# Two layers of a hybrid backbone: the S5 chunk tables' TensorE products issued as whole runs

## The chip, the cores and the metric

The kernel runs on one core of a Trainium2 chip. The metric is the device time of one execution in microseconds (us). A difference of about 0.5% (5.6 us) is what a measurement of this kernel can tell from no change.

## What is computed

Two layers of a backbone run on 384 tokens (128 of context, 256 of a latent grid) of width 1024. Each layer is a modulated RMS norm, one input projection, four parallel mixers, one output projection, a second norm and a gated MLP with a width-3 convolution:

```python
def trunk_layer(x, cvec, p, mixer_fn):
    sh1, sc1, g1, sh2, sc2, g2 = ada_mods(cvec, p)
    mixed, extra = mixer_fn(rmsnorm(x, p['norm1_g']) * (1 + sc1) + sh1)
    x = x + g1 * mixed
    x = x + g2 * conv_ffn(rmsnorm(x, p['norm2_g']) * (1 + sc2) + sh2, p)
    return x, extra

def mixers_context(h, p):
    na_z, s5_u, gq_z, mla_z = split_proj(h @ p['w_in'])
    o_na = attend(nq, nk, nv, NA_DH ** -0.5)
    o_s5, s5_state = s5_mixer(s5_u, p, ...)
    o_gq = attend(gq, gk, gv, GQ_DH ** -0.5)
    o_mla = attend(mq, mk, mv, MLA_QK ** -0.5)
    return concat(o_na, o_s5, o_gq, o_mla) @ p['w_out'], ...
```

The change touches the S5 mixer only: a state space of 16 channel groups with 64 complex states each, in two directions. The kernel computes it in chunks of eight tokens, which needs three tables per layer that depend on the weights alone: E (inputs of a chunk to its end state), F (start state to outputs) and KT (the lags inside a chunk).

## The kernel before

**Tiling.** Features lie on the 128 partitions, tokens on the free axis. Every large product is split in three products of single-pass floats (high by high, high by low, low by high), lines 295 to 297 in `mm3`: a weight tile of 128x128 against 384 or 386 columns. They fill the whole array of TensorE. The text calls them main products. Weights come in pieces by DMA; `split1` (lines 282 to 289) makes the high part on ScalarE (L287) and the low part on VectorE (L288), up to four half pieces of 512 columns ahead.

**Stages.** Layer 0: norm and first products, four mixers interleaved by the letters of `SPEC`, output projection, MLP in two halves of 11 pairs (`ffn`, lines 1310 to 1380). Then layer 1, the same. The S5 tables of layer 0 are made inside the mixers of layer 0, those of layer 1 inside the second MLP half of layer 0 (lines 1314 to 1322), at a lower priority (`LOWP`) than the MLP around them.

**The tables** (`s5_tables`, lines 687 to 734) are made in four blocks per layer. In each block VectorE makes `eb` by six operations (L491 to L500); TensorE transposes it twice (i = 0, 1) in four pieces of 128x128 (L707) into a PSUM tile, ScalarE copies it out (L708) and GpSimd's queue writes it to memory (L709). VectorE makes `ca` by six more operations (L491 to L498), which GpSimd's queue writes (L716). Then 16 products of 64 rows by 32 columns and 128 moving columns (L723) fill two PSUM tiles: four groups g on four strips of 32 columns, two directions d on the upper and lower 64 rows, and two parts i (real, imaginary) that are summed. The eight pairs of g and d stand on eight different corners of the array; i = 0 and i = 1 use the same corner one after the other. ScalarE (L727, L728) and VectorE (L729, L730) take the result to `KT`.

**Order.** Only the norm stage of layer 0 is written in its order by hand. Elsewhere a scheduler places the instructions of each engine in one fixed order at build time, by data dependences and priorities (`high_priority` raises one). The engines then run their orders and wait for each other by semaphores. `adjacent` (lines 242 to 247) traces the last of a list of products first and ties the others behind it with `issue_after`, so that they come after it; before the change it is used for column sums (L391, L903) and for the products of probabilities and values (L974, L978), and does not raise their priority.

**Small products beside these.** The modulation product (L318) uses 128 rows by 32 columns with 256 moving columns, four column strips at a time.

Of the kernel before, what the change touches and what calls it, by code (L numbers as in the profile page):

```python
# [34 lines left out]
PRL = 1000  # L35
PRX = 3000
NI = 0
NX = 5
# [177 lines left out]
def _program(tc, I, O):  # L216
# [25 lines left out]
    def adjacent(calls):  # L242
        """products of different column groups in a row, behind the last one"""
        calls[-1]()
        with tc.issue_after(nc.cur_bb.bb.instructions[-1]):
            for c in calls[:-1]:
                c()
# [90 lines left out]
    def step(n=1):  # L338
        """the next pieces of the modulation product"""
        for _ in range(n):  # L340
            if not ada_cur:
                if not ada_todo:
                    return
                ada_cur.append(ada_steps(*ada_todo[0]))
            next(ada_cur[0])
            left[0] -= 1
            if left[0] % 16 == 0:
                ada_cur.clear()
                ada_todo.pop(0)
# [10 lines left out]
    def rsqrt(src, scale, shape):  # L360
        """1 / sqrt(scale * src + EPS)"""
        xe = tiny(shape, "rs", 7)
        V.tensor_scalar(xe, src, scale, EPS, op0=OP.mult, op1=OP.add)
        xh = tiny(shape, "rs", 7)
        V.tensor_scalar(xh, xe, -0.5, None, op0=OP.mult)
        i = tiny(shape, "rs", 7, I32)
        V.tensor_scalar(i, xe.bitcast(I32), 1, None, op0=OP.logical_shift_right)
        yi = tiny(shape, "rs", 7, I32)
        V.tensor_scalar(yi, i, -1.0, float(0x5f3759df), op0=OP.mult, op1=OP.add)
        y = yi.bitcast(F32)  # L370
        for _ in range(3):
            t = tiny(shape, "rs", 7)
            V.tensor_tensor(t, y, y, op=OP.mult)
            V.tensor_tensor(t, t, xh, op=OP.mult)
            y2 = tiny(shape, "rs", 7)
            V.scalar_tensor_tensor(y2, t, 1.5, y, op0=OP.add, op1=OP.mult)
            y = y2
        return y
# [16 lines left out]
    def inv_rms(st, between=lambda i: None):  # L395
        """per token 1 / rms, the same on all rows of a psum tile"""
        ste = kp.tile([128, T], F32, name="ste", tag="sq", bufs=5)
        A.activation(ste, st[:, :T], AF.Copy)
        tr = pt()
        for b in range(3):  # L400
            PE.transpose(tr[:, 128 * b:128 * b + 128], ste[:, 128 * b:128 * b + 128], ident)
        ms = tiny((3,))
        V.tensor_reduce(ms, tr[:, :T].rearrange("p (b r) -> p b r", b=3)[:, :, 0:128:32], axis=AX.X, op=OP.add)
        A.activation(ms, ms, AF.Sqrt, scale=1.0 / D, bias=eps)
        between(0)
        r = tiny((3,))
        V.reciprocal(r, ms)
        between(1)
        bc = pt()
        for b in range(3):  # L410
            PE.transpose(bc[:, 128 * b:128 * b + 128], r[:, b:b + 1].to_broadcast([128, 128]), ident)
        return bc
# [23 lines left out]
    def unscaled(pool, tag, bufs, l, k, Am, sh):  # L436
        """x * gain in two parts, not yet over its rms, and the two shifts in columns behind it"""
        hi, lo = [pool.tile([128, 386], F32R, name="u" + t, tag=t, bufs=bufs) for t in tag]
# [11 lines left out]
    def scaled(out, z, bc, o1=0, o2=0):  # L450
        """product of unscaled() over the rms, with the shifts' product added; segment s at column o_s"""
        with tc.high_priority(offset=PRX):
# [16 lines left out]

# [1 line left out]
    lre, lim, ldt = s5p[:, 0], s5p[:, 1], s5p[:, 2]  # L471
# [35 lines left out]
    def par(*gens):  # L507
        """steps of independent chains in turn"""
        gens = list(gens)
# [7 lines left out]
    def s5_params(qp, rest):  # L517
        """powers of the discrete poles and input gains, one small instruction per step"""
        def tt(dt=F32, n=iter(range(99))):
# [126 lines left out]
    def s5_rot(l, w, w4, qp, cmp):  # L646
        """rotation by chunk position, decays, rotated entry states"""
        lg = slice(16 * l, 16 * l + 16)
# [38 lines left out]
    def s5_tables(l, qp, cmp, bc, dd):  # L687
        """chunk tables of one layer: E (inputs to end state), F (start state to outputs), lags inside a chunk"""
        lg = slice(16 * l, 16 * l + 16)
# [6 lines left out]
        for b in range(4):  # L696
# [6 lines left out]
            for i in range(2):  # L703
                e = kp.tile([128, 512], F32, name="tbo", tag="sqz", bufs=3)
                tr = pt()
                for g in range(4):
                    PE.transpose(tr[:, 128 * g:128 * g + 128], eb[:, i, g].rearrange("p j c -> p (j c)"), ident)  # L707
                A.activation(e, tr, AF.Copy)  # L708
                G.dma_start(SE[l][:, b, 512 * i:512 * i + 512], e)  # L709
# [8 lines left out]
            kd = [pt(), pt()]  # L718
            for d in range(2):
                h = slice(64 * d, 64 * d + 64)  # L720
                for i in range(2):
                    for g in range(4):
                        PE.matmul(kd[d][32 * g:32 * g + 32, 0:128], bb[i][h, 4 * b + g],  # L723
                                  ca[h, i, g, 2 * d:2 * d + 8].rearrange("p t c -> p (t c)"), start=i == 0,
                                  stop=i == 1)
            k4 = [k[:, 0:128].rearrange("p (t c) -> p t c", t=8) for k in kd]
# [9 lines left out]
    def s5_stream(l, st):  # L736
        """leaves 2 * gelu(y), channels on partitions, then the gated output"""
        with tc.tile_pool(name=f"sp{l}", bufs=1) as sp_:
# [160 lines left out]
    def stats(items, w=T):  # L899
        """column sums of squares; item c gives rows 32c.. by its weights; then [token, block, 32c + row]"""  # L900
        n = 32 * len(items)
# [16 lines left out]
    def softmax_unit(at, S, w, scale, bias, norm_act):  # L918
        """rows of exp(scale * S + bias - max) over their sum"""
        P = at.tile([128, T], F32, name="P", tag="P", bufs=3)  # L920
# [19 lines left out]
    def heads_stream(at, heads, res):  # L940
        """two heads, outputs on rows 0..63 and 64..127 of one tile, split in two parts"""
        PTs = []
# [44 lines left out]
    def kbroadcast(at, rr):  # L987
        """rr [128 tokens, block, 2] to rows of a psum tile, 64 rows each"""
        rb = at.tile([128, 3, 2, 64], F32, name="rb", tag="rp", bufs=1)
# [307 lines left out]
    def ahead(wsrc, n, H, zs, sts):  # L1297
        """first products of a stage from unscaled rows, then 1 / rms while they run"""
        bc = None
# [82 lines left out]
    def first(up, steps, rest):  # L1382
        """first layer: modulation, norm and the first products, rows k at a time; steps: DVE work between"""
        steps = [steps]
# [192 lines left out]
```

## Time and profile before

| what | value |
|---|---|
| time of three runs | 1115.03, 1115.62, 1119.07 us; median 1115.62 |
| profiled execution, first to last instruction | 1119.8 us (no other time is recorded for it) |
| TensorE busy | 1075.4 us, 96% of the span |
| VectorE busy | 803.6 us, 72% |
| ScalarE busy | 584.5 us, 52% |
| GpSimd busy | 86.0 us, 8% |
| DMA moved | 182.19 MB, 163 GB/s on average |

The span of the profiled execution is 4.2 us above the median of the runs. TensorE is the engine that is nearly always busy, but busy is not the same as doing useful work: the records of neighbouring products overlap, and the distance from the start of one product to the start of the next tells what it really costs. A record count of x2 for a small product (L723, L318) is one product in two passes, so x16 are eight products.

### The profile page before, as it was taken

The page shows a single profiled execution, that of the slowest core. Times are in us where ns is not written, and L with a number is a line of the kernel's source. Part 1 is how long each engine was busy: PE and PEld are TensorE (multiplying, and loading weights), DVE is VectorE, ACT ScalarE, POOL GpSimd, SP SyncE. Part 2 cuts the span into 40 slices and gives each one's busy share as a digit, 9 for nine tenths or more (in the row PEclk, how much of TensorE's full clock was granted, in tenths as well). Part 3 has the DMA queues.
Part 4 walks back from the last instruction along what each step waited for, and adds up shares of the span by engine and source line. Part 5 has one row for each costly group of instructions (what it writes and reads, how often), then busy time and mean ns, then how long its engine had stood idle before and what let it go on. Part 6 is the DMA issues. An engine that isn't in the chain of part 4 may idle for free.

```text
span 1119.8 us, 18705 instructions
## 1 busy us (share of the span) xinstructions
PE 1075.4 (96%) x6724; PEld 911.0 (81%) x6724; DVE 803.6 (72%) x2026; ACT 584.5 (52%) x1251; POOL 86.0 (8%) x197
## 2 busy tenths in 40 slices
PE   6789899999999999999999989899999999999998
PEld 3567575458889999996999887645699999999998
DVE  6888587867799854775976886567669875477753
ACT  3654445565675533552556644574567653355532
POOL 4213121000100000000010220000000000000000
PEclk8999899999999999998999998999999999999999
DMA  9978876464544444442455683336333434444343
GB/s 346 296 246 306 224 214 241 162 230 148 166 151 132 135 116 146 131 117 97 146 150 160 187 277 131 77 126 217 101 126 96 142 109 118 141 129 132 104 137 99
DMA packets 64700, 182.19 MB, mean 163 GB/s; under 512 B 15840, under 2 KB 19168, under 8 KB 64608
## 3 DMA queue, kind: packets, MB, share of 16 engines
q1 hardware_dynamic: 55456, 152.52, 44.0%
q0 software_dynamic: 8576, 28.16, 8.1%
q8 instruction: 53, 0.87, 0.3%
q10 hardware_dynamic: 576, 0.32, 0.1%
q14 instruction: 39, 0.32, 0.1%
HBM read 166.19 MB, written 14.78 MB: 162 GB/s over the span
## 4 chain that ended last, share of the span: by engine, by line
PE 67%; DVE 3%; DMA 1%; issue 1%; ACT 1%; POOL 0%; SPq 0%; DVEq 0%; POOLq 0%; ACTq 0%
PE pz L295 11%; PE pz L296 10%; PE pz L297 10%; PE psc L297 8%; PE psc L295 8%; PE psc L296 8%; PE pa L318 2%; PE psc L955 1%; PE ptr L723 1%; DMA bias<-rpb 1%; PE ptr L959 1%; DVE lo L288 1%; PE po L974 1%; PE psc L778 1%; DVE mg L798 0%
## 5 line engine op out<-in xcount | busy, mean ns | idle before, releaser
L287 ACT ACTIVATE hi<-raw 128x512 fp32r<-128x512 f32 (+2 forms) x396 | 228.3, 585 | 288.1 <-PE pz L296 120.0
L288 DVE TENSOR_TENSOR lo<-raw,hi 128x512 fp32r<-128x512 f32 (+2 forms) x396 | 252.6, 640 | 157.9 <-ACT hi L287 112.6
L295 PE MATMUL pz<-ah,hi 128*128 128x386 f32 (+1 forms) x616 | 216.3, 353 | 2.7 <-ACT ah L1439 1.7
L296 PE MATMUL pz<-al,hi 128*128 128x386 f32 (+1 forms) x616 | 213.7, 347 | 1.0 <-DVE al L426 1.0
L297 PE MATMUL pz<-ah,lo 128*128 128x386 f32 (+1 forms) x616 | 212.9, 346 | 0.1
L295 PEld LDWEIGHTS pz<-ah,hi 128*128 128x128 f32 x616 | 117.8, 191 | 21.6 <-issue 15.0
L296 PEld LDWEIGHTS pz<-al,hi 128*128 128x128 f32 x616 | 118.5, 192 | 7.0 <-issue 6.0
L297 PEld LDWEIGHTS pz<-ah,lo 128*128 128x128 f32 x616 | 118.0, 192 | 5.5 <-issue 4.4
L297 PE MATMUL psc<-ah,lo 128*128 128x386 f32 (+1 forms) x336 | 115.4, 343 | 0.1
L296 PE MATMUL psc<-al,hi 128*128 128x386 f32 (+1 forms) x336 | 115.1, 343 | 0.0
L295 PE MATMUL psc<-ah,hi 128*128 128x386 f32 (+1 forms) x336 | 115.1, 343 | 0.0
L295 PEld LDWEIGHTS psc<-ah,hi 128*128 128x128 f32 x336 | 64.1, 191 | 1.4 <-issue 1.0
L297 PEld LDWEIGHTS psc<-ah,lo 128*128 128x128 f32 x336 | 64.1, 191 | 0.9 <-DVE lo L288 0.4
L296 PEld LDWEIGHTS psc<-al,hi 128*128 128x128 f32 x336 | 64.0, 191 | 0.6 <-issue 0.6
L318 PE MATMUL pa<-raw,cw 128*32 128x256 f32 x640 | 59.1, 392 | 4.4 <-DMA raw<-ada 4.4
L295 PE MATMUL pz<-fh,hi 128*128 128x384 f32 x176 | 59.8, 340 | 0.0
L295 PE MATMUL psc<-fh,hi 128*128 128x384 f32 x176 | 59.4, 338 | 0.0
L297 PE MATMUL psc<-fh,lo 128*128 128x384 f32 x176 | 59.4, 337 | 0.0
L297 PE MATMUL pz<-fh,lo 128*128 128x384 f32 x176 | 59.3, 337 | 0.0
L296 PE MATMUL psc<-fl,hi 128*128 128x384 f32 x176 | 59.2, 336 | 0.0
L296 PE MATMUL pz<-fl,hi 128*128 128x384 f32 x176 | 59.1, 337 | 0.0
L932 ACT ACTIVATE P<-psc,ty 128x384 f32<-128x384 f32 (+1 forms) x56 | 32.3, 577 | 35.4 <-DVE ty L931 27.7
(431 smaller groups left out, 1959.7 us busy)
## 6 DMA issues: line engine op xcount, KB each, us to landing
raw<-wup SPq DMA_DIRECT2D x88, 512.0 KB, 3.6
raw<-ada SPq DMA_DIRECT2D x80, 512.0 KB, 4.5
raw<-win SPq DMA_DIRECT2D x30, 512.0 KB, 4.7
raw<-wdn SPq DMA_DIRECT2D x32, 384.0 KB, 3.1
raw<-wdn SPq DMA_DIRECT2D x32, 320.0 KB, 2.9
a<-ada SPq DMA_DIRECT2D x16, 512.0 KB, 6.2
raw<-wout SPq DMA_DIRECT2D x16, 512.0 KB, 3.7
se<-tbo POOLq DMA_DIRECT2D x16, 256.0 KB, 4.1
```

The lines of the kernel that those rows point to most:

```text
L287: A.activation(hi[:, :n], raw[:, a:b], AF.Copy)
L288: V.tensor_tensor(lo[:, :n], raw[:, a:b], hi[:, :n].bitcast(F32), op=OP.subtract)
L295: PE.matmul(out, wh, xh, start=start, stop=False)
L296: PE.matmul(out, wh, xl, start=False, stop=False)
L297: PE.matmul(out, wl, xh, start=False, stop=stop)
L318: PE.matmul(acc[32 * c:32 * c + 32, 256 * h:256 * h + 256], cw[:, kc], raw[:, 256 * c:256 * c + 256], start=kc == 0 and h == 0, stop=kc == ...
L723: PE.matmul(kd[d][32 * g:32 * g + 32, 0:128], bb[i][h, 4 * b + g], ca[h, i, g, 2 * d:2 * d + 8].rearrange("p t c -> p (t c)"), start=i == ...
L778: PE.matmul(e[:, NC * q:NC * q + NC], E[:, 128 * q:128 * q + 128], U[:, 4 * b + g], start=True, stop=True)
L932: A.activation(P[:, :w], S[:, :w], AF.Exp, bias=mx, scale=scale, accum_out=rs)
L955: PE.matmul(S[:, :T], qf(1 + qb), kf(128, 512), start=True, stop=True)
L959: PE.transpose(tr[:, 128 * kb:128 * kb + 128], P[:, 128 * kb:128 * kb + 128], ident)
L974: calls.append(lambda kb=kb, j=j: PE.matmul(o[64 * j:64 * j + 64, 128:T], heads[j][2](1 + kb), PTs[j][1][:, kb].rearrange("p q c -> p (q c ...
```

## The change

`adjacent` now raises the priority of all its products but the last one traced (`PRA` = 6000). The transposes of a table and the products of the lags are handed to it: the four transposes of an `eb` half as one run, and all 16 lag products as one run. The order of the lag products turns round: first i = 1 for all groups and directions, then i = 0, with the direction as the innermost loop, so that upper and lower rows take turns. No instruction is added or removed. Seventeen lines of comments are taken out beside this.

```diff
+PRA = 6000
...
     def adjacent(calls):
         calls[-1]()
-        with tc.issue_after(nc.cur_bb.bb.instructions[-1]):
+        with tc.issue_after(nc.cur_bb.bb.instructions[-1]), tc.high_priority(offset=PRA):
             for c in calls[:-1]:
                 c()
...
             for i in range(2):
                 e = kp.tile([128, 512], F32, name="tbo", tag="sqz", bufs=3)
                 tr = pt()
-                for g in range(4):
-                    PE.transpose(tr[:, 128 * g:128 * g + 128], eb[:, i, g].rearrange("p j c -> p (j c)"), ident)
+                adjacent([lambda g=g: PE.transpose(tr[:, 128 * g:128 * g + 128],
+                                                   eb[:, i, g].rearrange("p j c -> p (j c)"), ident)
+                          for g in range(4)])
...
             kd = [pt(), pt()]
-            for d in range(2):
-                h = slice(64 * d, 64 * d + 64)
-                for i in range(2):
-                    for g in range(4):
-                        PE.matmul(kd[d][32 * g:32 * g + 32, 0:128], bb[i][h, 4 * b + g],
-                                  ca[h, i, g, 2 * d:2 * d + 8].rearrange("p t c -> p (t c)"), start=i == 0,
-                                  stop=i == 1)
+            calls = []
+            for i in (1, 0):
+                for g in range(4):
+                    for d in range(2):
+                        h = slice(64 * d, 64 * d + 64)
+                        calls.append(lambda i=i, g=g, d=d, h=h: PE.matmul(
+                            kd[d][32 * g:32 * g + 32, 0:128], bb[i][h, 4 * b + g],
+                            ca[h, i, g, 2 * d:2 * d + 8].rearrange("p t c -> p (t c)"), start=i == 1, stop=i == 0))
+            adjacent(calls[1:] + calls[:1])
```

The rows below are the instruction orders of the two kernels. In the changed kernel line numbers are higher: main products are L296 to L298, the modulation product is L319, the lag products are L726, the two additions to `KT` are L733 and L734. The names `bb_5240` and `bb_5241` (layer 1) and `bb_878` and `bb_879` (layer 0) are the parts i = 0 and i = 1.

TensorE in the second MLP half of layer 0, the tables' first block for layer 1, before:

```order
L723 MATMUL ptr<-ca,bb_5240 32x128
L295 MATMUL pz<-ah,hi 128x386
L723 MATMUL ptr<-ca,bb_5240 32x128
L296 MATMUL pz<-al,hi 128x386
L723 MATMUL ptr<-ca,bb_5241 32x128
L297 MATMUL pz<-ah,lo 128x386
L723 MATMUL ptr<-ca,bb_5241 32x128
L295 MATMUL pz<-ah,hi 128x386
```

The same place in the changed kernel:

```order
L298 MATMUL psc<-ah,lo 128x386
L707 MATMUL ptr<-cst,eb 128x128 x8
L296 MATMUL pz<-ah,hi 128x386
L297 MATMUL pz<-al,hi 128x386
L298 MATMUL pz<-ah,lo 128x386
L296 MATMUL pz<-ah,hi 128x386
L297 MATMUL pz<-al,hi 128x386
L298 MATMUL pz<-ah,lo 128x386
L296 MATMUL pz<-ah,hi 128x386
L726 MATMUL ptr<-ca,bb_5241 32x128 x8
L726 MATMUL ptr<-ca,bb_5240 32x128 x8
L297 MATMUL pz<-al,hi 128x386
```

Before, single lag products and main products took turns; now the 16 lag products of a block stand together. Over the whole program the 128 lag products stood in 37 places (24 of one product, 13 of eight) and now stand in 8 places of 16. The 64 transposes stood in 25 places and now stand in 15.

TensorE in the mixers of layer 0, the tables' first block for layer 0, before:

```order
L295 MATMUL pz<-ah,hi 128x384
L723 MATMUL ptr<-ca,bb_879 32x128 x8
L296 MATMUL pz<-al,hi 128x384
L297 MATMUL pz<-ah,lo 128x384
L318 MATMUL pa<-raw,cw 32x256 x8
L295 MATMUL pz<-ah,hi 128x384
```

The same place in the changed kernel:

```order
L298 MATMUL pz<-ah,lo 128x384
L319 MATMUL pa<-raw,cw 32x256
L726 MATMUL ptr<-ca,bb_879 32x128 x8
L726 MATMUL ptr<-ca,bb_878 32x128 x8
L319 MATMUL pa<-raw,cw 32x256 x7
L296 MATMUL pz<-ah,hi 128x384
```

Here each part i already stood as a run of eight; the part i = 0 moved from 13 main products earlier to stand with i = 1, and the run now parts a set of eight modulation products in one and seven. This happens in two of layer 0's four blocks.

VectorE at the first block for layer 1, where it takes the lag products' results, before:

```order
L1350 TENSOR_TENSOR af<-cv 128x256
L496 TENSOR_TENSOR cm_5323<-PQ_98,bb_5240 128x512
L1354 TENSOR_TENSOR fl<-af,fh 128x384
L729 TENSOR_TENSOR KT<-ptr,s5dd 128x16
L500 TENSOR_TENSOR eb<-cm_5322,cm_5323 128x512
L288 TENSOR_TENSOR lo<-raw,hi 128x512
L1342 SCALAR_TENSOR_TENSOR cv<-pz,vec,cv 128x385
L730 TENSOR_TENSOR KT<-ptr,KT 128x16
```

The same place in the changed kernel:

```order
L1354 TENSOR_TENSOR af<-cv 128x256
L733 TENSOR_TENSOR KT<-ptr,s5dd 128x16
L497 TENSOR_TENSOR cm_5323<-PQ_98,bb_5240 128x512
L289 TENSOR_TENSOR lo<-raw,hi 128x512
L1358 TENSOR_TENSOR fl<-af,fh 128x384
L734 TENSOR_TENSOR KT<-ptr,KT 128x16
L501 TENSOR_TENSOR eb<-cm_5322,cm_5323 128x512
```

The two additions to `KT` stand a little earlier among VectorE's work, and `eb` of the next block still follows them. Elsewhere the mixers of layer 0 (the stretch from about 56 to 280 us) are put in another order on TensorE, VectorE and ScalarE, with most instructions moved by under 20 places; from the mixers of layer 1 on the orders agree but for a few rows. GpSimd's order and SyncE's each differ in 6 rows.

## Rows read from the trace of the kernel before

**Rows 1.** The page: busy time by engine, and granted TensorE clock in 40 slices.
```profile
PE 1075.4 (96%) x6724; PEld 911.0 (81%) x6724; DVE 803.6 (72%) x2026; ACT 584.5 (52%) x1251; POOL 86.0 (8%) x197
PEclk8999899999999999998999998999999999999999
```

**Rows 2.** Windows: stretch, its length, busy us by engine, granted clock, DMA.
```profile
450.00:500.80 50.80, 50.80 (x290) 50.80 (x289) 36.75 (x66) 26.93 (x48) 0.00 (x0) 1.00 0.43 125
500.80:565.60 64.80, 64.80 (x404) 51.27 (x402) 49.61 (x91) 26.98 (x53) 6.48 (x11) 0.95 0.38 117
516.70:519.60 2.90, 2.90 (x10) 2.88 (x10) 1.43 (x3) 0.60 (x2) 0.00 (x0) 0.50 0.01 3
531.80:565.60 33.80, 33.80 (x263) 31.15 (x262) 32.91 (x61) 16.81 (x35) 3.40 (x6) 1.00 0.45 140
```

**Rows 3.** Timeline of TensorE, layer 1's tables: start us, us, instruction, count.
```profile
500.83 0.34 PE L297 MATMUL psc<-ah,lo 128*128 128x386 f32 x1
501.01 0.60 PE L707 MATMUL ptr<-cst,eb 128*128 128x128 f32 x4
501.36 0.42 PE L295 MATMUL pz<-ah,hi 128*128 128x386 f32 x1
501.62 0.27 PE L707 MATMUL ptr<-cst,eb 128*128 128x128 f32 x1
501.65 0.42 PE L296 MATMUL pz<-al,hi 128*128 128x386 f32 x1
...
504.29 0.40 PE L723 MATMUL ptr<-ca,bb 64*32 64x128 f32 x2
...
504.99 0.40 PE L723 MATMUL ptr<-ca,bb 64*32 64x128 f32 x2
...
528.97 0.40 PE L723 MATMUL ptr<-ca,bb 64*32 64x128 f32 x2
```

**Rows 4.** The same view, where the granted clock is halved.
```profile
514.56 0.63 PE L723 MATMUL ptr<-ca,bb 64*32 64x128 f32 x2
...
515.74 0.63 PE L723 MATMUL ptr<-ca,bb 64*32 64x128 f32 x2
...
516.78 0.53 PE L297 MATMUL psc<-ah,lo 128*128 128x386 f32 x1
...
519.68 0.42 PE L707 MATMUL ptr<-cst,eb 128*128 128x128 f32 x1
```

**Rows 5.** The same view, a run of eight lag products among main products.
```profile
531.53 0.34 PE L297 MATMUL psc<-ah,lo 128*128 128x386 f32 x1
531.80 0.45 PE L723 MATMUL ptr<-ca,bb 64*32 64x128 f32 x16
...
532.47 0.34 PE L296 MATMUL psc<-al,hi 128*128 128x386 f32 x1
```

**Rows 6.** The same view, four modulation products (682 us) and eight (71 us).
```profile
682.47 0.33 PE L297 MATMUL pz<-ah,lo 128*128 128x384 f32 x1
682.73 0.64 PE L318 MATMUL pa<-raw,cw 128*32 128x256 f32 x8
...
683.58 0.34 PE L296 MATMUL pz<-al,hi 128*128 128x384 f32 x1
```

**Rows 7.** The same view, layer 0: the eight modulation products, and two waits.
```profile
70.83 0.34 PE L297 MATMUL pz<-ah,lo 128*128 128x384 f32 x1
71.10 1.07 PE L318 MATMUL pa<-raw,cw 128*32 128x256 f32 x16
...
72.39 0.34 PE L296 MATMUL pz<-al,hi 128*128 128x384 f32 x1
...
120.65 0.72 PE L318 MATMUL pa<-raw,cw 128*32 128x256 f32 x8 [2.81 <-DMA raw<-ada]
```

**Rows 8.** Waits of TensorE from 56 to 280 us: total us, times, longest.
```profile
PE ptr L723 <- DVE ca L493: 2.2, 1, 2.2
```

**Rows 9.** Timeline of VectorE, a wait for the lag products' results in layer 0.
```profile
97.65 0.17 DVE L729 TENSOR_TENSOR KT<-ptr,s5dd 128x16 f32<-128x16 f32 x1 [1.33 <-ACT KT L727]
```

## The prediction

> **What bounds the kernel now.** I read the page first: TensorE is busy 96% of the span, VectorE 72%, ScalarE 52% [rows 1], so the question for each stretch is whether TensorE waits there, and if not, what its time is made of. The windows around the tables of layer 1 come next. From 450.0 to 500.8 us, plain MLP products, TensorE starts 290 products in 50.8 us, 0.176 us apart at a granted clock of 1.00 [rows 2]. That is the price of one main product. From 500.8 to 565.6 us, the stretch with the tables, TensorE is again busy without a gap, and no wait of TensorE is to be seen there. It is the bound, and the excess over 0.176 us per main product is what the tables cost.
>
> The timeline shows where the excess comes from. The lag products of the first block and half of the second stand singly between main products: one starts at 504.29 and the next, one main product later, at 504.99 [rows 3]. The pair takes 0.70 us, so a single lag product costs 0.70 - 0.18 = 0.52 us. There are 24 such singles, from 504.29 to 528.97. A run of eight lag products costs hardly more: from the main product at 531.53 to the second one behind the run at 532.47 are 0.94 us, less two main products 0.59 us [rows 5]. So the price is almost all in going over to the small tiles and back, and the eight corners work side by side.
>
> The singles have a second cost. [...] There a pair takes 1.18 us (514.56 to 515.74), and nine main products from 516.78 to 519.68 take 0.322 us each [rows 4].
>
> **The change, part by part.**
>
> *Lag products of layer 1, what goes.* 21 singles at full clock cost 21 x 0.52 = 10.9 us. Three at the lower clock cost 3 x (1.18 - 0.18) = 3.0 us. The nine main products behind them lose 9 x (0.322 - 0.176) = 1.3 us. The other 40 products stand in five runs of eight, 5 x 0.59 = 2.9 us. Together 18.1 us.
>
> *Lag products of layer 1, what comes.* Four runs of 16. The trace of before has none. From below a run costs what eight cost, 0.59 us, if the second eight hide; from above as two runs, 1.18 us. For a second set on the same corners the nearest row is the modulation product: four products of 256 columns cost 683.58 - 682.47 - 2 x 0.176 = 0.76 us [rows 6], eight cost 72.39 - 70.83 - 2 x 0.176 = 1.21 us [rows 7]. The second set adds 0.45 us at 256 columns, so about 0.22 us at 128. I take 0.59 + 0.22 = 0.81 us, four times 3.2 us (2.4 to 4.7). The gain on TensorE is 18.1 - 3.2 = 14.9 us (13.4 to 15.7). All of it lies on the path, because TensorE never waits in this stretch.
>
> I count the clock's share, 3 x (1.18 - 0.70) + 1.3 = 2.7 us, as gained: the long stretch of singles ahead of the fall is gone.
>
> *Transposes.* Four in a run make the distance from 500.83 to 501.36, less one main product 0.35 us, and the next product is still 0.11 us late; a single one makes 501.36 to 501.65, less one main product 0.11 us, four of them 0.46 us [rows 3]. Full-size tiles need no run. I cost this part at nothing.
>
> *Who is waited for next.* The work of VectorE stays, and its stretch gets shorter. From 500.8 to 565.6 us VectorE is busy 49.6 us [rows 2]; the stretch falls from 64.8 to about 64.8 - 14.9 = 49.9 us. VectorE would be full. From 531.8 to 565.6 it already works 32.91 of 33.80 us, 97%, and TensorE did not wait [rows 2]; at 97% the 49.6 us need 51.1 us. I give back 1.2 us (0 to 1.2 in this case), with the four half pieces that VectorE may be ahead as cover. If that cover is gone, rival A holds.
>
> *Layer 0.* Eight runs of eight, 8 x 0.59 = 4.7 us, become four of 16, 3.2 us. Two of them part a set of modulation products, which go over to another tile shape once more, 0.76 - 0.45 = 0.31 us each. The gain of 0.9 us does not reach the end: at 120.65 us TensorE waits 2.81 us for the modulation weights' DMA [rows 7], and arriving earlier makes that wait longer. The wait of 2.2 us for `ca` [rows 8] moves from i = 0 to the whole run, which needs i = 1 as well; it was the first to come, the run comes later, so I leave it. I cost layer 0 at 0, with 3 us to either side for the changed order of the mixers, which no row prices.
>
> *Priorities and queues.* The other users of `adjacent` (column sums, values) already stood in whole runs and still do. No DMA is added; the tables' stores on GpSimd's queue follow their producers, earlier if anything. The next layer reads the tables only in its mixers, well behind.
>
> *Sum.* -14.9 + 1.2 + 0 = -13.7 us. The profiled execution would go from 1119.8 to 1106.1 us. Its span stands 4.2 us above the median of the runs; the same difference on 1115.6 gives **1101.9 us**. Should the runs without a profile not have had the fall of the clock, it is 2.7 us less, 1104.6.
>
> **The rivals.**
>
> *A. VectorE becomes the bound in the tables' stretch.* For it: 49.6 us of work in 49.9. Its chain also goes through TensorE and back (lag products, ScalarE's copy, the additions to `KT`, then the next `eb`), and VectorE works in a fixed order: in layer 0 it waited 1.33 us for such a copy [rows 9]. One such wait in each of four blocks, 5.3 us, has no free time left to fall into. Against it: TensorE did not wait at 97%. The time would be 1101.9 + 5.3 = 1107.2 us. [...]
>
> *B. Slower: taking upper and lower rows in turn keeps the products apart.* The runs of eight in the trace have four products on one half and then four on the other; the new order changes halves, and PSUM tiles, at every product. No row shows that. If each change cost what a single one costs, a run would take 16 x 0.52 = 8.3 us, eight runs 66.6 us against 18.1 + 4.7 = 22.8 us now: 1115.6 + 43.8 = 1159 us. It decides from 22.8 / 8 = 2.9 us per run upward. Against it: in the run of eight the one change of half is not to be seen, as eight cost 0.59 and one 0.52. [...]
>
> *C. The mixers of layer 0 lose what the tables gain.* The order of 56 to 280 us is another one, and every engine follows it rigidly. For it: small moves there have already led to waits of 2.8 and 2.2 us [rows 7, 8]. Two more such waits are 5.0 us, and a fall of the clock behind them, as priced above, 1.3 us: 1101.9 + 6.3 = 1108.2 us, and with three of them no change. Against it: most instructions move by under 20 places, and two waits could as well go.
>
> That the change does not do what it says is ruled out by the order: eight places of 16 are there.
>
> **How the numbers follow.** Forecast 0.68, A 0.15, C 0.12, B 0.05. The forecast's own bounds are 1115.6 - 15.7 - 3 = 1097 and 1104.6 + 1.5 = 1106 us (runs of 16 at their dearest). The range goes down to 1096 and up to 1109, which takes in A and about half of C and leaves out B. Faster by over 0.5% (5.6 us, about what a measurement of this kernel can tell from no change) means under 1110.0: forecast, A and half of C, 0.89. Within 0.5%: the other half of C, 0.06. Slower: B, 0.05.
>
> **What would show it.** In the changed kernel's profile the eight runs should each cost 0.6 to 1.2 us between main products; no lag product should stand alone; the granted clock should stay at 1.00 in the 50 us of layer 1's tables; that stretch should take 50 to 51 us for the same products, with VectorE busy 97% or more of it. Waits of TensorE for `ca`, `eb` or weights' low parts there, of over 3 us in total, would show rival A. Runs of 3 us or more would show B. If the tables' stretch gains its 14 us and the total does not, the mixers of layer 0 have lost it (C).

## The result, and the profile after

The changed kernel took 1105.37 us (median of four runs, 1103.95 to 1108.5), the kernel before beside it 1115.71 us (four runs, 1115.03 to 1119.07). The ratio is 0.9886, with a 95% interval of 0.9857 to 0.9915: 12.7 us less by the ratio (9.5 to 16.0), 10.3 us less by the medians. The change is faster, as forecast (0.89); the time lies in the range, 3.5 us above the forecast of 1101.9.

The page of the changed kernel, its span, busy times and granted clock in 40 slices, to be laid beside [rows 1]:

```profile
span 1103.5 us, 18695 instructions
PE 1059.3 (96%) x6724; PEld 904.8 (82%) x6724; DVE 801.5 (73%) x2026; ACT 582.4 (53%) x1251; POOL 85.5 (8%) x197
PEclk8999998999999999999999999999999999999999
```

The profiled span fell by 16.3 us, and TensorE's busy time by 16.1 us, with the same 6724 instructions. The whole count fell from 18705 to 18695, but no engine's row of busy instructions changed. The 8 of the slice from 504 to 532 us, the fall of the clock among the singles (to 0.50 [rows 2]), is gone. The 8 at 672 us is gone too, but a second execution of the kernel before lacks it as well, so that one is not the change's. To find where the time went, I compared the start of the n-th main product in both traces, since their order hardly changes in the MLPs:

| from main product to main product | before, us | after, us | difference |
|---|---|---|---|
| 0 to 1700 (layer 0 up to the tables of layer 1) | 476.7 | 475.4 | -1.3 |
| 1700 to 2000 (the tables of layer 1) | 75.6 | 61.4 | -14.2 |
| 2000 to 2300 (rest of the MLP, start of layer 1) | 61.0 | 61.0 | 0.0 |
| 2300 to 2800 (mixers of layer 1) | 209.7 | 208.0 | -1.7 |
| 2800 to 4300 | 265.7 | 265.7 | 0.0 |

Product 0 itself starts 0.8 us later after the change. So all of the gain that is more than the scatter between two executions lies in the tables of layer 1. Windows of the changed kernel: first from product 1700 to 2000, then the same main products as the stretch of 64.8 us in [rows 2] (1703 to 1944); columns as there:

```profile
499.80:561.10 61.30, 60.68 (x461) 56.97 (x460) 55.31 (x108) 31.86 (x65) 10.03 (x15) 1.00 0.54 163
500.30:551.20 50.90, 50.35 (x403) 46.87 (x401) 49.03 (x92) 26.47 (x53) 7.07 (x11) 1.00 0.46 149
```

The 64.8 us have become 50.6 (from 500.28 to 550.91), at a granted clock of 1.00. VectorE is busy 49.03 of 50.9 us, 96%, and TensorE idles hardly at all.

Timeline of TensorE in the changed kernel, the run of 16 of the second block, which answers to the singles of [rows 3] and the eight of [rows 5]:

```profile
516.57 0.34 PE L298 MATMUL psc<-ah,lo 128*128 128x386 f32 x1
516.84 0.67 PE L726 MATMUL ptr<-ca,bb 64*32 64x128 f32 x32
517.44 0.44 PE L296 MATMUL psc<-ah,hi 128*128 128x386 f32 x1
517.72 0.34 PE L297 MATMUL psc<-al,hi 128*128 128x386 f32 x1
```

From 516.57 to 517.72 are 1.15 us; less two main products, 16 lag products cost 0.80 us. The others cost the same within 0.1 us.

Waits of TensorE in the changed kernel, from 499.8 to 561.1 us (total, times, longest):

```profile
PE ptr L707 <- DVE KT L734: 0.3, 1, 0.3
PE ptr L707 <- DVE eb L501: 0.2, 1, 0.2
```

The three longest waits of VectorE in the same stretch of the kernel before (500.3 to 575.9 us):

```profile
DVE lo L288 <- ACT hi L287: 8.4, 11, 1.9
DVE KT L730 <- ACT KT L728: 3.2, 1, 3.2
DVE KT L729 <- ACT KT L727: 3.0, 1, 3.0
```

and the longest after:

```profile
DVE lo L289 <- ACT hi L288: 3.8, 7, 1.4
```

TensorE waits 0.5 us for the tables. VectorE has no wait at all for the lag products' copies any more: when the 16 products come together, both PSUM tiles are complete together. Before, the singles of the first block spread them out; ScalarE's two copies of that block started 6.7 us apart, each behind a wait for lag products (timeline of ScalarE before):

```profile
509.68 0.26 ACT L727 ACTIVATE KT<-ptr 128x112 f32<-128x112 f32 x1 [3.28 <-PE ptr L723]
516.40 0.26 ACT L728 ACTIVATE KT<-ptr 128x112 f32<-128x112 f32 x1 [3.56 <-PE ptr L723]
```

### The profile page after: what moved, and what is told of

Read it like the earlier page. It is cut to its first block, busy times and chain, and to the rows that moved or that the text cites. A ratio compares the mean times of both kernels' runs of the same rounds, so it can differ in the third digit from the quotient of the medians.

```text
span 1103.5 us, 18695 instructions
## 1 busy us (share of the span) xinstructions
PE 1059.3 (96%) x6724; PEld 904.8 (82%) x6724; DVE 801.5 (73%) x2026; ACT 582.4 (53%) x1251; POOL 85.5 (8%) x197
## 4 chain that ended last, share of the span: by engine, by line
PE 65%; DVE 4%; DMA 2%; ACT 1%; issue 0%; POOL 0%; SPq 0%; DVEq 0%; POOLq 0%; ACTq 0%
PE pz L296 11%; PE pz L297 10%; PE pz L298 10%; PE psc L298 8%; PE psc L297 8%; PE psc L296 8%; PE pa L319 2%; PE psc L959 1%; DVE lo L289 1%; DMA bias<-rpb 1%; PE ptr L963 1%; PE po L978 1%; DMA tbw<-sw 1%; PE psc L782 0%; DMA sw<-rw 0%
## 5 line engine op out<-in xcount | busy, mean ns | idle before, releaser
L296 PE MATMUL pz<-ah,hi 128*128 128x386 f32 (+1 forms) x616 | 213.8, 348 | 1.4 <-ACT gs L882 0.8
L297 PE MATMUL pz<-al,hi 128*128 128x386 f32 (+1 forms) x616 | 210.8, 343 | 1.0 <-DVE al L427 1.0
L298 PE MATMUL pz<-ah,lo 128*128 128x386 f32 (+1 forms) x616 | 210.2, 341 | 0.1
L296 PEld LDWEIGHTS pz<-ah,hi 128*128 128x128 f32 x616 | 116.5, 189 | 18.9 <-issue 13.4
L298 PEld LDWEIGHTS pz<-ah,lo 128*128 128x128 f32 x616 | 116.7, 190 | 3.0 <-issue 2.2
L296 PE MATMUL psc<-ah,hi 128*128 128x386 f32 (+1 forms) x336 | 114.2, 340 | 0.0
L298 PE MATMUL psc<-ah,lo 128*128 128x386 f32 (+1 forms) x336 | 113.9, 339 | 0.1
L319 PE MATMUL pa<-raw,cw 128*32 128x256 f32 x640 | 62.5, 393 | 3.5 <-DMA raw<-ada 3.5
L296 PEld LDWEIGHTS psc<-ah,hi 128*128 128x128 f32 x336 | 63.5, 189 | 0.7 <-issue 0.4
L298 PEld LDWEIGHTS psc<-ah,lo 128*128 128x128 f32 x336 | 63.4, 189 | 0.4 <-DVE lo L289 0.4
L296 PE MATMUL pz<-fh,hi 128*128 128x384 f32 x176 | 59.4, 338 | 0.1
L298 PE MATMUL pz<-fh,lo 128*128 128x384 f32 x176 | 59.5, 338 | 0.0
L296 PE MATMUL psc<-fh,hi 128*128 128x384 f32 x176 | 59.3, 337 | 0.0
L298 PE MATMUL psc<-fh,lo 128*128 128x384 f32 x176 | 59.3, 337 | 0.0
```

What stands on the lines that cost most here:

```text
L296: PE.matmul(out, wh, xh, start=start, stop=False)
L297: PE.matmul(out, wh, xl, start=False, stop=False)
L298: PE.matmul(out, wl, xh, start=False, stop=stop)
L319: PE.matmul(acc[32 * c:32 * c + 32, 256 * h:256 * h + 256], cw[:, kc], raw[:, 256 * c:256 * c + 256], start=kc == 0 and h == 0, stop=kc == ...
```

## Experiments

Twelve kernels were run, in three sets, each set on one chip beside its own runs of the kernel before. These took 1120.3, 1119.8 and 1121.5 us (medians), with runs from 1112 to 1126 us; only ratios are compared across sets. Line numbers shift by a few from kernel to kernel.

The theory: the gain is the price of 24 changes of shape and back, and of the clock that falls among them. The rivals: layer 0's changed order takes part of it back (C); corners in turn, or the transposes, have a price or a gain of their own.

### The kernel before, again

The kernel before, with no edit but a constant that nothing reads:

```diff
+VARIANT = 2
```

> The kernel before, unchanged, once more with a profile. It shows how far one execution differs from the next. Theory 1 (the profiled execution of before was an ordinary one): a span of about 1119.8 us, with the granted clock at its lower level for some 6 us behind the single lag products of layer 1 (513.5 to 520). Theory 2 (that execution was a slow one of its kind): a span of 1113 to 1116 us, with fewer falls of the clock, and the fall behind the singles either there (then 2.7 us of the gain are the clock's in ordinary runs too) or not (then the gain of the change in ordinary runs is 11 to 12 us, not 14).

Measured: 1118.74 us (10 runs), ratio 0.999 (0.9955 to 1.0024). Window of this trace from main product 1700 to 2000:

```profile
499.30:574.90 75.60, 75.60 (x462) 61.62 (x462) 56.17 (x109) 32.39 (x65) 10.03 (x15) 0.95 0.44 132
```

The 75.6 us and the fall of the clock (0.95 over the stretch) are there again. A second execution agrees to 0.1 us. Its span was 1117.2 us, between what the two theories asked for.

### Layer 1 alone, layer 0 alone

The lag products and transposes of one layer as runs, those of the other loose as before (`l in (1,)` here, `(0,)` in the second); the column sums and values keep the priority that they had before.

```diff
-            for d in range(2):
-                for i in range(2):
-                    for g in range(4):
-                        PE.matmul(...)
+            if l in (1,):
+                calls = [lambda i=i, g=g, d=d: lag(i, g, d, 1)
+                         for i in (1, 0) for g in range(4) for d in range(2)]
+                adjacent(calls[1:] + calls[:1], True)
+            else:
...
```

> Only the tables of layer 1 as whole runs; layer 0's tables and its mixers in the order of before. Theory 1 (all of the gain comes from the 24 single lag products of layer 1): 11.5 to 14.5 us under before, so 1101 to 1104 us, and no slower than the whole change. Theory 2 (the new order of layer 0's mixers gave something too): less gain than the whole change, 1107 us or more.

> Only the tables of layer 0 as whole runs; those of layer 1 as before, singles and all. Theory 1: no gain, and by the changed trace, in which layer 0's MLP began 2.6 us later, a loss of 1 to 4 us: 1116 to 1120 us. Theory 2: a gain of 2 us or more. The runs of 16 should cost 0.8 us each in either case.

Measured: layer 1 alone 1103.7 us (4 runs), ratio 0.9862 (0.9823 to 0.99), main product 1700 to 2000 in 61.4 us. Layer 0 alone 1128.83 us (7 runs), ratio 1.0086 (1.0059 to 1.0113): slower. Its trace, from main product 1700 to 2000, then from 0 to 1700, then a part of layer 0's mixers:

```profile
506.80:582.10 75.30, 75.30 (x462) 61.65 (x461) 56.13 (x109) 32.50 (x65) 10.04 (x15) 0.95 0.44 133
25.40:506.80 481.40, 458.69 (x2990) 376.99 (x2987) 363.59 (x934) 254.38 (x549) 46.10 (x93) 0.98 0.60 186
180.00:210.00 30.00, 24.00 (x122) 12.39 (x122) 16.74 (x48) 11.79 (x32) 1.63 (x3) 0.89 0.56 183
```

and the timeline of TensorE there, a modulation product before its weights have landed:

```profile
186.20 1.06 PE L320 MATMUL pa<-raw,cw 128*32 128x256 f32 x2 [3.77 <-DMA raw<-ada]
```

All the gain is layer 1's. Layer 0 alone lost 8.5 us by the medians, where its expectation had a loss of 1 to 4 us at most. Layer 0 took 481.4 us instead of 476.7. One place of the loss is the row above: the scheduler had put a modulation product where TensorE must stand 3.77 us for its weights, and the granted clock is down around it (0.89 over the 30 us). This is rival C's mechanism, but not the change's own order: without the raised priority of the column sums and values the scheduler makes another order of layer 0 than the change's. The next set has the right comparison.

### Layer 0 in exactly the order of the change; layer 1 and the whole change, again

The first kernel differs from the one with layer 1 alone by the lines below (the second stands in two places). The other two are the kernel with layer 1 alone and the changed kernel, unedited.

```diff
-    def adjacent(calls, pri=False):
+    def adjacent(calls, pri=True):
...
-            if l in (1,):
+            if l in (0,):
```

> Layer 0 alone, in exactly the order that the whole change gives the norm and the mixers of layer 0 on TensorE (the earlier run of layer 0 alone left out the raised priority of the column sums and values and so got another order of its own); layer 1's tables stay as before the change, 24 singles and the fall of the clock. Theory 1 (the changed order of layer 0's mixers costs time by more waits and a fall of the clock): from the 100th to the 600th main product about 237 us as in the whole change, against 232.5 in the kernel before; the total 2 to 4 us above before, ratio 1.002 to 1.004. Theory 2 (this order costs nothing, the 237 us were chance): 232 to 233 us there, ratio 1.000 within 0.002. Both: the tables' stretch of layer 1 keeps its 75.5 us (main product 1700 to 2000).

> The runs in layer 1's tables alone, once more, beside the whole change on the same chip. If layer 0's part costs 2 to 4 us, this kernel is faster than the whole change by that much, ratio 0.985 to 0.987 against 0.988 to 0.990 for the whole; if it costs nothing, the two agree within 1 us.

> The whole change once more, unchanged. Ratio to before 0.988 to 0.990 if layer 0's part takes 2 to 4 us of the 14 us back; 0.987 (as layer 1 alone) if it takes nothing.

Measured, with shared runs of the kernel before (17): layer 0 in the change's order 1119.39 us, ratio 1.000 (0.9974 to 1.0025); layer 1 alone 1104.86 us, 0.9867 (0.9839 to 0.9896); the whole change 1107.47 us, 0.989 (0.9858 to 0.9921). Theory 1 of the first expectation is nearly right on its 237 us (235.6 from the 100th to the 600th main product) and wrong on the total; the 75.5 us that both theories expected in layer 1's tables did not come either. Windows of the first kernel, from main product 0 to 1700 and from 1700 to 2000:

```profile
23.90:499.70 475.80, 455.72 (x2990) 376.62 (x2987) 362.92 (x934) 254.53 (x549) 46.01 (x93) 0.98 0.59 188
499.70:572.00 72.30, 72.30 (x462) 59.57 (x461) 56.07 (x108) 32.48 (x65) 10.04 (x15) 1.00 0.46 137
```

Two things follow. First, part of what layer 0's new order loses up to the 600th main product is not lost at all. The kernel before has, behind that product, a wait of TensorE in the norm that follows (from 299.1 to 500.3 us):

```profile
PE ptr L411 <- DVE ty L407: 2.4, 1, 2.4
PE pz L296 <- DVE al L426: 1.0, 1, 1.0
```

The changed kernel has only the second one there. TensorE comes later, so it waits no more for VectorE in the norm. (This wait is 2.4, 2.1 and 1.7 us in three executions of the old order and there in none of the three of the new one.) From 0 to 1700 the three executions in the new order (after, this one, the whole change again) took 475.4, 475.8 and 477.0 us, mean 476.1; eight executions in the old order 473.9 to 476.7, mean 475.0. TensorE's order from 0 to 1700 is the same, row for row, within each of the two groups. The cost is about 1 us, which is no more than two executions of one order differ. The difference between the whole change and layer 1 alone (0.989 against 0.9867 here, 0.9886 against 0.9862 before) points the way of a cost of 2 to 4 us both times, but the intervals overlap; it is not settled.

Second, in this execution the clock did not fall in the tables. TensorE's order between main products 1700 and 2000 is row for row that of the kernel before, 24 singles and all, and the stretch takes 72.3 us instead of 75.6, with no wait of TensorE in either. That prices the fall, 3.3 us, and leaves 72.3 - 61.4 = 10.9 us for the change of the order alone. Timeline of TensorE in this kernel, for comparison with the pairs of 1.18 us in [rows 4]:

```profile
513.55 0.40 PE L728 MATMUL ptr<-ca,bb 64*32 64x128 f32 x2
513.88 0.44 PE L297 MATMUL psc<-ah,hi 128*128 128x386 f32 x1
514.25 0.40 PE L728 MATMUL ptr<-ca,bb 64*32 64x128 f32 x2
```

A pair takes 0.70 us here, as at 504 us.

### The inside of a run: same corner twice, halves apart

With layer 1 alone, only the order of the 16 calls was changed; first the two parts i one after the other on each corner, then four upper and four lower rows as a block:

```diff
-                         for i in (1, 0) for g in range(4) for d in range(2)]
+                         for g in range(4) for d in range(2) for i in (1, 0)]
```

```diff
-                         for i in (1, 0) for g in range(4) for d in range(2)]
+                         for i in (1, 0) for d in range(2) for g in range(4)]
```

> The runs in layer 1's tables alone, but inside a run the two products of a corner (i = 1, then i = 0, summed in the same place) follow each other at once; everything else is in the order of the run with layer 1 alone. Theory 1 (the eight corners work side by side, and a second product on a corner waits for the first): eight pairs that each add about 0.22 us on top of 0.59, some 2.3 us per run instead of 0.80; the stretch from main product 1700 to 2000 takes 4 x 1.5 = 6 us more than 61.3. Theory 2 (a product costs its start only, wherever it stands): 0.80 us per run, 61.3 us.

> The runs in layer 1's tables alone, but inside a run the four products of the upper rows come first and the four of the lower rows then, for i = 1 and again for i = 0, as the eights stood before the change. Theory 1 (the change between upper and lower rows costs nothing): 0.80 us per run as with turns. Theory 2 (rival B in a small size: a turn costs something): under 0.70 us per run, 61.3 less 0.4 us or more.

Measured: 1103.48 and 1104.28 us (one run each), and main product 1700 to 2000 in 61.4 and 61.3 us. Timeline of TensorE, same corner twice:

```profile
515.00 0.34 PE L299 MATMUL psc<-ah,lo 128*128 128x386 f32 x1
515.27 0.71 PE L728 MATMUL ptr<-ca,bb 64*32 64x128 f32 x32
515.91 0.44 PE L297 MATMUL psc<-ah,hi 128*128 128x386 f32 x1
516.19 0.34 PE L298 MATMUL psc<-al,hi 128*128 128x386 f32 x1
```

and with the halves apart:

```profile
515.95 0.34 PE L299 MATMUL psc<-ah,lo 128*128 128x386 f32 x1
516.22 0.67 PE L728 MATMUL ptr<-ca,bb 64*32 64x128 f32 x32
516.82 0.44 PE L297 MATMUL psc<-ah,hi 128*128 128x386 f32 x1
517.10 0.34 PE L298 MATMUL psc<-al,hi 128*128 128x386 f32 x1
```

Same corner twice costs 1.19 - 0.35 = 0.84 us, halves apart 1.15 - 0.35 = 0.80 us. A turn between halves costs nothing that shows, so rival B has no ground. And the 2.3 us of theory 1 did not come: products that follow each other on a corner cost 0.04 us more per run.

### Lag products alone, transposes alone

With layer 1 alone, one of the two `adjacent` calls was taken back; in the first kernel that of the transposes:

```diff
-                    adjacent(tcs, True)
+                    for c in tcs:
+                        c()
```

in the second that of the lag products:

```diff
-                adjacent(calls[1:] + calls[:1], True)
+                for d in range(2):
+                    for i in range(2):
+                        for g in range(4):
+                            lag(i, g, d, 0)
```

> Only the 16 lag products of layer 1's blocks as runs; the transposes stay one by one where the order puts them (12 singles). Theory 1 (full-size transposes cost nothing more when they stand singly): the stretch from main product 1700 to 2000 takes 61.3 us within 0.5, the total as with layer 1 alone, ratio 0.985 to 0.988. Theory 2 (a single transpose costs a share of a change of shape): 12 x 0.1 to 0.3 us, 62.5 to 65 us, ratio 0.988 to 0.990.

> Only the transposes of layer 1's blocks as runs; the lag products stay loose, and the order puts them as 19 singles, one five and five eights. Theory 1 (all of the gain is the lag products): against 24 singles 5 x 0.52 less 0.56 for the five, 2.0 us less, so 70.3 us from main product 1700 to 2000 without a fall of the clock and up to 73.6 with one. Theory 2 (the transposes' runs bring something of their own): under 69 us.

Measured: lag products alone 1103.15 us (4 runs), ratio 0.9861 (0.981 to 0.9912); transposes alone 1117.94 us (one run, beside a median of 1121.46). Windows from main product 1700 to 2000, lag products alone:

```profile
497.40:558.10 60.70, 60.50 (x463) 57.16 (x462) 55.27 (x109) 31.99 (x65) 10.07 (x15) 1.00 0.55 164
```

and transposes alone:

```profile
499.40:570.00 70.60, 70.39 (x461) 59.16 (x460) 56.20 (x108) 32.21 (x65) 10.03 (x15) 1.00 0.47 141
```

Without the transposes' runs the stretch is 0.7 us shorter rather than longer (60.7 us in one execution; all executions with both kinds of runs took 61.3 or 61.4). With them alone it takes 70.7 us, where the count of singles (19, one five, five eights) asked for 70.3 without a fall of the clock, and the clock did not fall. The transposes' part of the change brings nothing; it seems to cost the 0.7 us, as single transposes wait for nothing here and their runs wait 0.5 us for VectorE.

### The same edit elsewhere: modulation products as runs

The four products of a piece of modulation weights were handed to `adjacent` too, once on top of the whole change, once on top of layer 1 alone (there with the raised priority for them and the tables alone):

```diff
-                for c in range(4):
-                    PE.matmul(...)
+                adjacent([lambda c=c: PE.matmul(...) for c in (1, 2, 3, 0)])
```

> The whole change, and the four column strips of each modulation product tied to one run in the same way. In the changed kernel 320 of them stand in 79 places, 35 of them of one, two or three products, where the rest of the four stands elsewhere; now no place has fewer than four. If a place of small tiles costs 0.31 us by itself, as read from four and eight products, some 13 places fewer (79 to 68) save 3 to 4 us where TensorE is the bound: 1101 to 1103 us. If the mixers of layer 0 are held by waits and not by TensorE, nothing: 1104 to 1107 us.

> The runs in layer 1's tables alone, and beside them the four modulation products of a weight piece as one run (46 sets of four and 6 of twelve stand where 14 single ones, 12 of three and so on stood). Theory: splitting those sets costs about 0.3 us for each change of shape, some 15 to 20 fewer of them give 4 to 6 us on top of layer 1's 14: ratio 0.982 to 0.983, main product 2300 to 2800 in 202 to 203 us (206 without). Rival: layer 0's mixers, in an order 146 rows away from before, lose as much to waits for the modulation weights (3 to 8 us between main product 100 and 600): ratio 0.986 to 0.989, no better than layer 1 alone.

Measured: on the whole change 1107.08 us (4 runs), ratio 0.988 (0.9842 to 0.9918), no better than without. On layer 1 alone 1097.67 us (6 runs, 1091.84 to 1100.66), ratio 0.9792 (0.9762 to 0.9822): faster than both kernels of this study, and its interval lies below that of layer 1 alone. From main product 0 to 1700 in the first:

```profile
25.90:506.60 480.70, 455.32 (x2997) 374.49 (x2994) 363.09 (x934) 255.37 (x549) 45.56 (x93) 0.97 0.59 187
```

and in the second:

```profile
25.60:496.30 470.70, 450.73 (x2997) 375.40 (x2994) 362.06 (x934) 255.60 (x549) 45.64 (x93) 0.98 0.60 191
```

The edit is the same and the result is not: layer 0 took 480.7 us in one order and 470.7 in the other, against means of 476.1 and 475.0 without the edit. In the first kernel the expected place, the mixers of layer 1, did give 5 us (202.0 us against 208.0 and 206.9 in the whole change), and layer 0 took them back; in the second it gave little (206.2 us against 204.8 and 207.5 with layer 1 alone), while 202 to 203 were expected, but its trace has a fall of the clock there. The ratio gains 0.0075, some 8 us, over layer 1 alone, and the medians 7.2 us; the traced executions differ by 2.9 us only. They are not typical of their kernels: the one with the modulation runs took 1100.03 us at a mean granted clock of 0.981, 2.4 us above its median; the one with layer 1 alone 1102.94 us at 0.989, 1.9 us below its own. Window of the fall in the mixers of layer 1 (the trace with layer 1 alone has 1.00 between these times):

```profile
741.70:748.50 6.80, 6.80 (x28) 3.57 (x29) 4.76 (x9) 2.18 (x4) 0.00 (x0) 0.50 0.48 159
```

Which stages hold the gain in an ordinary execution, no trace here shows.

## Why the prediction was right, and where it was off

**What bounds the kernel.** Right. In layer 1's tables TensorE's own time was the price, and only 0.5 us of waits took its place.

**Lag products.** Right, and the sum held better than its terms had a right to. The forecast had 24 singles and five eights at full clock against four runs of 16, 24 x 0.52 + 2.9 - 3.2 = 12.2 us, less 1.2 us for VectorE, 11.0 us. The comparison without a fall of the clock gives 10.9 us. The run of 16 was put at 0.81 us and measured 0.80. Its reason was only half right: "a second set on the same corners" is not what adds the 0.2 us, since it makes little difference whether a product follows its own corner's or another's (0.84 against 0.80). That the sum agrees to 0.1 us is partly luck, as the 1.2 us were to be VectorE's at 97% and came in another way (below).

**The clock.** Here the step failed that counted its share as certainly gained. It was put at 2.7 us, from the pair and the nine main products of [rows 4] at a granted clock of 0.50 [rows 2], and measured 3.3 (75.6 - 72.3), but it is not there in every execution: three traces with 24 singles have it (before, before again, layer 0 alone; 0.95 each from main product 1700 to 2000) and one does not (1.00). The term left out the transposes and main products behind 519.68 us, where the granted clock is still 0.83 (519.6 to 522.0). The forecast for runs without the fall was 1104.6 us; 1105.4 was measured. How many of the plain runs had this fall isn't recorded. Their mean granted clock over the whole kernel is: of the 17 runs of the kernel before beside the repeats, the fastest (1112.28 us) had 0.989 and the slowest (1124.76 us) 0.974, so the scatter between runs goes with the clock; in which stages it fell they do not show.

**Profile and runs.** The sum for the profiled execution was 1106.1 us of span, measured 1103.5, so the sum itself asked for too little gain there. The error in the forecast of 1101.9 is in the 4.2 us taken off from there to the median. After the change the profiled execution has a span of 1103.5 and a time of 1105.24 us, 1.7 us above its span. If the same 1.7 us lay around the span before, that execution took about 1121.5 us, slower than all of its listed runs (the 1119.07 included), though not slower than the slowest of the later runs of that kernel (1112 to 1126 us). Part of its excess, the fall of the clock perhaps among it, was then not theirs to lose; that is argued from the times and not shown. A forecast from such an execution should have taken a smaller gain, not the same gain from a lower start. With the sizes measured since, 1115.6 - 10.9 + 1 is 1105.7.

**Transposes.** They were put at nothing, and they gained nothing; as runs they seem to cost 0.7 us (60.7 us without them), in waits for VectorE.

**VectorE.** The stretch was forecast at 50 to 51 us and took 50.6. VectorE was 96% full in it instead of 97% or more. Rival A did not come: the waits of TensorE there are 0.5 us, and VectorE's own 6.2 us of waits for the copies to `KT` went, because a block's lag products now end together. Of the 1.2 us given back for VectorE about as much was lost (12.2 - 10.9 = 1.3 us), 0.7 us of it with the transposes' runs. Emptying the PSUM tiles cost TensorE one wait of 0.3 us there, for the addition to `KT` (L734).

**Layer 0.** The total was right, 0 forecast with 3 us either way and about 1 us measured; its steps were not. The wait for `ca` stayed, as said (2.2 us, [rows 8]). The wait for the modulation weights was to grow by what the runs save, and that step failed: the waits on that DMA were 3.5, 3.9 and 4.1 us in total in the three executions of the new order, against 3.4 to 5.0 us in the eight of the old one. Four of the waits of TensorE in the changed kernel from 24.4 to 301.6 us:

```profile
PE pa L319 <- DMA raw<-ada: 3.5, 5, 1.2
PE psc L959 <- ACT P L930: 3.3, 1, 3.3
PE ptr L726 <- DVE ca L499: 2.2, 2, 2.0
PE pz L1218 <- ACT mk L1214: 1.4, 1, 1.4
```

The second row and the last are rival C's kind (before, they were 1.7 us and none). C was right in kind and wrong in amount for this order; two neighbouring orders lost about what it forecast (481.4 us with layer 0 alone and 480.7 with the modulation runs, instead of 475.0 and 476.1).

## What to carry to other kernels

Count the changes of tile shape between neighbouring instructions of TensorE, not the small products: here one small product between full-size ones cost 0.52 us and sixteen together 0.80. Full-size transposes (0.11 us for a single one [rows 3]) and turns between corners (0.80 us per run, with the halves in turn or apart) needed no such care here. When a scheduler redraws a distant stage beside the edit, confine the edit, or compare at a point of the program behind which the same work is done; a point inside that stage showed a loss of 4.6 us (product 100 to 600, 237.3 us against 232.7) where about 1 us was left at product 1700.

## What the runs showed of the hardware

A product of 64 rows by 32 columns and 128 moving columns, inside a run of its shape, adds 0.026 us ((0.80 - 0.59) / 8), while a full-size transpose of 128 moving columns adds 0.11 us [rows 3]. I had not expected that this nearly holds even when each corner gets its two products one right after the other (0.84 us for 16). A single product between full-size ones costs 0.52 us [rows 3], and turns between corners and halves inside a run cost nothing that shows (0.80 us either way).

The granted clock fell to 0.50 after some 9 us of singles, while TensorE's records show it busy without a gap. In all three traces with the fall it begins at the 14th single, 9.2 us after the first: there the distance to the next single is over 1 us instead of 0.70. In the kernel before, again:

```profile
511.77 0.40 PE L723 MATMUL ptr<-ca,bb 64*32 64x128 f32 x2
...
512.47 0.54 PE L723 MATMUL ptr<-ca,bb 64*32 64x128 f32 x2
...
513.56 0.63 PE L723 MATMUL ptr<-ca,bb 64*32 64x128 f32 x2
```

In one execution of four with the same singles it did not fall at all (1.00 from main product 1700 to 2000). Whether the same moment in the other three is chance, the traces cannot tell. What set the moment here stays open.
